# A hybrid decoder layer in which the scheduler orders every engine by its other machine model

## The chip, the cores and the metric

The kernel runs on one core of one Trainium2 chip. Its time is the device time of one execution in microseconds. Before the change it is 1043.64 us, the median of 3 runs (1043.46 to 1045.11). The core has five engines that run beside each other, each with a queue of its own that is worked off strictly in order: TensorE (PE, with its weight loads PEld), VectorE (DVE), ScalarE (ACT), GpSimd (POOL) and SyncE (SP, which here only starts DMAs). They wait for one another by semaphores.

## The reference

One layer over 272 tokens (16 meta tokens and 256 of the sequence), width 2048, in float32:

```
p = h @ W_in -> [q heads | latent kv | indexer q, key, weights | pool channels]
attn = top-64 sparse attention over the latent, T5 bias     (8 heads)
pool = trailing means of 2, 4, 8, 16 tokens less the token, a map per group
h = LN(alpha*h + concat(attn, pool) @ W_o)
z = causal depthwise conv, width 3, of (h @ W_up)           (2 x 5632 columns)
f = (gelu(a) * g) @ W_down                                  (a, g: halves of z)
out = LN(alpha*h + f) without the meta tokens
```

## The kernel before, in words

**Precision and the weight stream.** Every matmul operand is split into a high and a low half, and each product of a weight tile with an activation tile takes three matmuls: high x high (L202), high x low (L203), low x high (L204). All weights come as a stream of 128x2048 tiles of 1 MB. `fetch` (L146 to L163) starts the load of a tile into `wraw` on SP's queue (L149), has ACT copy its two halves of 1024 columns to high parts (L162) and DVE subtract for the low parts (L163), both into `whl`. The pool `wp` has three buffers for each. `weights(ahead=2)` asks for a tile two products before it is used. A load can begin only when the split of the tile three before it has freed `wraw`; a split needs a free `whl`, so the matmuls of the tile three before it must be done.

**Stages in time.** First the keys and latents, from tiles that bring x and weights together. Then 24 projection tiles and, between them, the indexer's dots and top-k, and per head `softmax`, `turn` (L492 to L509, transposes on PE and copies) and `values` (L511 to L520). Then 16 output tiles of W_o (`output`). The sums for LN1 are gathered by the way in `about_k` (L625 to L645; sums on POOL, L635 to L637).

**The folded products.** So that PE need not wait for LN1, the first eight products of the FFN, four columns tiles in two halves each (FOLDED = 4), run on the values before LN1, called `fold`, and are corrected afterwards. During the first of them PE also does the token sums (`deviation`, L244), DVE and POOL make 1/deviation and mean from them (L672 to L679), PE spreads these over the partitions (`deviation_rows`, L250), and ACT copies the spread rows to `rs` and `m2`, which the profile calls `of_token` (L685). After that:

```
def unfold(ps):
    nc.vector.tensor_copy(sc, ps[:, NQ:NE])                        # L719
    nc.vector.tensor_tensor(u, ps[:, :NQ], rs, op=ALU.mult)        # L721
    nc.scalar.activation(w, m2, AF.Identity, bias=sc[:, 1:], scale=sc[:, :1])
    nc.gpsimd.tensor_tensor(u, u, w, op=ALU.add)                   # L724
```

`unfold` reads a folded product's PSUM bank; L721 is the last to do so. There are four such banks (`pm`, tag mm), so a product's matmuls can start only when the unfold of the product four before it is through L721. The conv (ACT L711, DVE L712 and L713), the gate (L728, DVE L729) and the halves of the result (L734, L735) follow; `u` has two buffers. Meanwhile `normalise` makes the sixteen tiles of h for the products that come after: POOL L693 (x times rs), DVE L694 (plus m2), ACT, then DVE L698 (low half, tile `hp`). Sixteen 32x32-block transposes of the residual (L861, DVE) belong to the same stretch.

**The FFN** then alternates up tiles (48 matmuls of 258 columns) with down tiles, which follow a seven-product scheme in kinds A, B and C. A B tile is combined first (DVE L157 to L159) and has a split of 1024 and one of 512 columns. At the end of a group the products in PSUM are added on DVE (L791, L798 to L809) and by DMA.

**The end.** The last part's down product (`down`, L886 to L888) takes rows 0 to 127 in four banks, then rows 128 to 255 in five pieces (three of 512 columns, two of 256). DVE adds each piece to the residual (L892), ACT squares it (L895); the mean comes from the first three pieces (L914, L909) and the product with the weight sums; then (x - mean) g (L900) of all five pieces, the variance (L914, L968, L969), its power -1/2 on POOL (L929 for the first half of the rows, L970 for the second), and x rstd + b (L904) with the output DMAs (L905).

**What sets the order.** The kernel is written for a scheduler: the program's lines say what depends on what, in an order; the scheduler of `TileContext` then orders the instructions of every engine, hands out the pool buffers, and sets the semaphores. It does so by a model of the machine. L1034 opens this context.

## Time and profile before

| | |
|---|---|
| median of 3 runs | 1043.64 us |
| the profiled execution, time | 1044.78 us |
| its span in the profile | 1043.0 us |
| mean granted clock of TensorE | 0.996 |
| matmuls that PE ran, with the short ones | 7649 |
| weight splits on DVE, L163 | 492.8 us, 418 of 1214 ns |
| weight copies on ACT, L162 | 404.4 us, 418 of 1014 ns |
| HBM | 225 GB/s over the span |

A row of the timeline has start, length, engine, line, operation, the tile written and the tiles read (without buffer numbers), shapes and a count of equal operations in a row; in brackets the idle time of the engine before it and what ended it. In the windows each engine's busy time is followed by its count; the last three numbers are TensorE's granted clock (1 is full), the DMA engines' busy share and GB/s. Matmul ends are modelled and overlap, so the pace of PE is read from start to start.

### The profile page before, as it was taken

Reading aid. Unit: us, or ns where it says so; the run is one execution under the profiler, and the core shown is the slowest. Engines: PE = TensorE matmul, PEld = TensorE weight load, DVE = VectorE, ACT = ScalarE, POOL = GpSimd, SP = SyncE. Lnnn points to the kernel's source line nnn. Section 1 sums busy time; section 2 is a strip of 40 time slices with the busy share of each in tenths; the row PEclk is TensorE's granted clock in tenths of the full one; section 3 lists DMA queues with packets and bytes.
Section 4 is the critical chain, followed back from the end, with each engine's and each line's share of the span. In section 5 each row is a group of like instructions: output and inputs, shape, how many; then the busy total and the mean of one; then the engine's idle time right before and its main releaser. Section 6 shows DMA issues by size and latency. Waiting matters only on the chain.

```text
span 1043.0 us, 19170 instructions
## 1 busy us (share of the span) xinstructions
PE 1027.7 (99%) x7649; PEld 975.8 (94%) x7649; DVE 889.4 (85%) x1376; ACT 612.5 (59%) x987; POOL 204.1 (20%) x256
## 2 busy tenths in 40 slices
PE   9999999999999999999999999999999999999996
PEld 8998999999999999999999999999999999999885
DVE  6879468858879987898999999899899999899866
ACT  6666345645447765656566665556556665566543
POOL 1100014125445231201112021120111211111010
PEclk9999999999999999999999999999999999999998
DMA  8756542454552577899788787887879879788872
GB/s 320 260 177 232 197 157 94 142 196 163 198 202 82 202 219 213 268 301 296 264 274 298 290 277 268 292 281 277 277 268 301 282 270 296 267 277 285 306 230 82
DMA packets 59466, 249.75 MB, mean 239 GB/s; under 512 B 21702, under 2 KB 22384, under 8 KB 32368
## 3 DMA queue, kind: packets, MB, share of 16 engines
q1 hardware_dynamic: 34448, 230.15, 61.0%
q0 software_dynamic: 7600, 15.62, 7.9%
q10 hardware_dynamic: 17328, 2.75, 1.5%
q8 instruction: 60, 0.98, 0.4%
q14 instruction: 30, 0.25, 0.1%
HBM read 232.50 MB, written 2.11 MB: 225 GB/s over the span
## 4 chain that ended last, share of the span: by engine, by line
PE 78%; DVE 12%; DMA 4%; issue 2%; ACT 2%; POOL 1%; SPq 0%; DVEq 0%; POOLq 0%; ACTq 0%
PE mm L204 19%; PE mm L203 19%; PE mm L202 19%; PE at L784 5%; PE at L785 5%; PE at L783 5%; DVE whl L163 5%; DMA wraw<-in_w_down 1%; DMA wraw<-in_w_up 1%; ACT whl L162 1%; DMA wraw<-in_w_first 1%; DVE hp L698 1%; DVE x L694 1%; DMA wraw<-in_w_proj 0%; DVE za L712 0%
## 5 line engine op out<-in xcount | busy, mean ns | idle before, releaser
L163 DVE TENSOR_TENSOR whl<-wraw,whl 128x1024 fp32r<-128x1024 f32 (+1 forms) x418 | 492.8, 1214 | 53.6 <-ACT whl L162 51.0
L162 ACT ACTIVATE whl<-wraw 128x1024 fp32r<-128x1024 f32 (+1 forms) x418 | 404.4, 1014 | 142.1 <-DVE wraw L158 41.3
L204 PE MATMUL mm<-hp,whl 128*128 128x258 f32 x1280 | 361.6, 282 | 0.8 <-DVE whl L163 0.8
L203 PE MATMUL mm<-hp,whl 128*128 128x258 f32 x1280 | 360.3, 281 | 0.0
L202 PE MATMUL mm<-hp,whl 128*128 128x258 f32 x1280 | 356.3, 278 | 0.7 <-ACT whl L162 0.7
L202 PEld LDWEIGHTS mm<-hp,whl 128*128 128x128 f32 x1280 | 241.4, 189 | 4.1 <-ACT whl L162 0.9
L203 PEld LDWEIGHTS mm<-hp,whl 128*128 128x128 f32 x1280 | 240.4, 188 | 3.1
L204 PEld LDWEIGHTS mm<-hp,whl 128*128 128x128 f32 x1280 | 241.0, 188 | 1.0 <-DVE whl L163 1.0
L202 PE MATMUL mm<-xp,whl 128*128 128x256 f32 (+5 forms) x384 | 110.4, 287 | 0.0
L204 PE MATMUL mm<-xp,whl 128*128 128x256 f32 (+5 forms) x384 | 108.4, 282 | 0.5 <-DVE whl L163 0.5
L203 PE MATMUL mm<-xp,whl 128*128 128x256 f32 (+5 forms) x384 | 108.2, 282 | 0.0
L783 PE MATMUL at<-whl,gp 128*128 128x512 f32 x212 | 83.5, 394 | 0.5 <-DVE u L808 0.5
L784 PE MATMUL at<-whl,gp 128*128 128x512 f32 x212 | 83.7, 395 | 0.1
L785 PE MATMUL at<-whl,gp 128*128 128x512 f32 x212 | 83.5, 394 | 0.0
L203 PEld LDWEIGHTS mm<-xp,whl 128*128 128x128 f32 x384 | 72.2, 188 | 0.8 <-issue 0.5
L204 PEld LDWEIGHTS mm<-xp,whl 128*128 128x128 f32 x384 | 72.1, 188 | 0.9 <-DVE whl L163 0.9
L202 PEld LDWEIGHTS mm<-xp,whl 128*128 128x128 f32 x384 | 72.2, 188 | 0.6
L711 ACT ACTIVATE z<-mm,cv 128x256 f32<-128x256 f32 x40 | 22.6, 565 | 77.5 <-PE mm L204 77.5
L751 POOL TENSOR_TENSOR forms<-za 128x128 f32<-128x128 f32 x20 | 19.1, 955 | 223.8 <-DVE za L729 216.3
L711 ACT ACTIVATE za<-mm,cv 128x256 f32<-128x256 f32 x40 | 22.5, 562 | 47.4 <-PE mm L204 44.2
L785 PEld LDWEIGHTS at<-whl,gp 128*128 128x128 f32 x212 | 39.8, 188 | 9.2
L783 PEld LDWEIGHTS at<-whl,gp 128*128 128x128 f32 x212 | 39.8, 188 | 8.8 <-DVE u L808 1.0
(307 smaller groups left out, 1850.3 us busy)
## 6 DMA issues: line engine op xcount, KB each, us to landing
wraw<-in_w_up SPq DMA_DIRECT2D x88, 1024.0 KB, 5.1
wraw<-in_w_down SPq DMA_DIRECT2D x80, 1024.0 KB, 6.4
wraw<-in_w_proj SPq DMA_DIRECT2D x24, 1024.0 KB, 4.9
wraw<-in_w_o SPq DMA_DIRECT2D x16, 1024.0 KB, 4.9
y<-v POOLq DMA_DIRECT2D x27, 256.0 KB, 9.2
y<-u POOLq DMA_DIRECT2D x18, 256.0 KB, 4.6
wraw<-in_w_first SPq DMA_DIRECT2D x9, 304.0 KB, 5.3
x<-in_xt SPq DMA_DIRECT2D x1, 2176.0 KB, 8.7
```

The lines of the kernel that those rows point to most:

```text
L162: nc.scalar.activation(hl[:, 0, c], raw[:, c], AF.Copy)
L163: nc.vector.tensor_tensor(hl[:, 1, c], raw[:, c], hl[:, 0, c].bitcast(F32), op=ALU.subtract)
L202: nc.tensor.matmul(ps, wh, ah, start=n == 0, stop=False)
L203: nc.tensor.matmul(ps, wh, al, start=False, stop=False)
L204: nc.tensor.matmul(ps, wl, ah, start=False, stop=n == KT - 1)
L694: nc.vector.tensor_tensor(yd, yd, m2, op=ALU.add)
L698: nc.vector.tensor_tensor(a[:, 1, :NQ], yd, a[:, 0, :NQ].bitcast(F32), op=ALU.subtract)
L711: nc.scalar.activation(z, src[:, 2:NQ], AF.Identity, bias=col(C_B, j), scale=col(C_W, 3 * j + 2))
L751: nc.gpsimd.tensor_tensor(s[:, 3], a11, a21, op=ALU.subtract)
L783: nc.tensor.matmul(ps, a[:, 0, i], hl[:, 0, w], start=fresh, stop=False)
L784: nc.tensor.matmul(ps, a[:, 0, i], hl[:, 1, w], start=False, stop=False)
L785: nc.tensor.matmul(ps, a[:, 1, i], hl[:, 0, w], start=False, stop=last)
```

## The change

One argument is added where the scheduler's context is opened:

```
-    with tile.TileContext(nc) as tc:
+    with tile.TileContext(nc, schedule_with_timeline_sim=True) as tc:
         tile_layer(tc, *args)
```

The scheduler orders all engines' instructions by its other model of the machine, the one that follows queues and transfers in time. No line of the computation changes; every engine has the same operations, in another order, with other buffers of the pools and so other waits. Three places follow as they stand in the two programs (the number behind a name tells buffers apart).

**TensorE, the first folded product.** `st` holds 1/deviation and mean; the two spreads L250 of them are read by ACT as rs and m2. Before, they follow each other:

```order
L203 MATMUL mm<-fold,whl 128x260
L204 MATMUL mm<-fold,whl 128x260
L250 MATMUL at<-ident,st 128x128 x2
L250 MATMUL at<-ident,st 128x2
L250 MATMUL at<-ident,st 128x128 x2
L250 MATMUL at<-ident,st 128x2
L202 MATMUL mm<-fold,whl 128x260
```

Now, at the same step:

```order
L202 MATMUL mm<-fold,whl 128x260
L250 MATMUL at<-ident,st 128x128 x2
L250 MATMUL at<-ident,st 128x2
L203 MATMUL mm<-fold,whl 128x260
L204 MATMUL mm<-fold,whl 128x260
L202 MATMUL mm<-fold,whl 128x260
L203 MATMUL mm<-fold,whl 128x260
L204 MATMUL mm<-fold,whl 128x260
L250 MATMUL at<-ident,st 128x128 x2
L250 MATMUL at<-ident,st 128x2
L202 MATMUL mm<-fold,whl 128x260
```

The spreads are five matmuls apart, and both are later: counted from the first matmul on `fold`, before there are 21 matmuls, the sums L244 (twice three), 21 matmuls, and the spreads; now 36, three L244, 6, three L244, 37, three L250, 5 and three L250.

**VectorE, the unfold of the fourth folded product.** mm_4070 is the bank that the eighth folded product takes next, u_4149 what L721 writes. Before:

```order
L163 TENSOR_TENSOR whl_4064<-wraw_4063,whl_4064 128x1024 x2
L698 TENSOR_TENSOR hp_4122<-x_1154,hp_4122 128x258
L698 TENSOR_TENSOR hp_4128<-x_1154,hp_4128 128x258
L719 COPY sc_4147<-mm_4070 128x2
L721 TENSOR_TENSOR u_4149<-mm_4070,of_token_2766 128x258
L861 STREAM_TRANSPOSE x_1154<-x_1154 128x256
L698 TENSOR_TENSOR hp_4134<-x_1154,hp_4134 128x258
```

Now:

```order
L713 SCALAR_TENSOR_TENSOR z_3983<-u_3978,cv_191,z_3983 128x256
L163 TENSOR_TENSOR whl_4236<-wraw_4235,whl_4236 128x1024
L861 STREAM_TRANSPOSE x_1154<-x_1154 128x256
L698 TENSOR_TENSOR hp_4232<-x_1154,hp_4232 128x258
L861 STREAM_TRANSPOSE x_1154<-x_1154 128x256
L698 TENSOR_TENSOR hp_4294<-x_1154,hp_4294 128x258
L163 TENSOR_TENSOR whl_4321<-wraw_4320,whl_4321 128x1024 x2
L729 TENSOR_TENSOR za_3789<-za_3789,z_3983 128x256
L721 TENSOR_TENSOR u_4149<-mm_4070,of_token_2766 128x258
L712 SCALAR_TENSOR_TENSOR za_3789<-u_4139,cv_191,za_3789 128x256
```

L721 stood behind the splits of whl_4064; now it stands behind those of whl_4162, whl_4236 and whl_4321, three weight tiles further on, and behind fourteen of the transposes L861, of which none was ahead of it before. In the same way u_4139, which empties the third product's bank, stands behind both splits of whl_4162 now, and before behind those of whl_3990.

**VectorE, the end.** y2 is the residual, at_11602, at_11625 and at_11641 are the third, fourth and fifth piece, few holds mean and rstd. Before:

```order
L892 SCALAR_TENSOR_TENSOR y2_3788,row_sums_11478<-y2_3788,at_11602 128x512
L914 TENSOR_REDUCE few_11480<-row_sums_11478 128x1
L892 SCALAR_TENSOR_TENSOR y2_3788,row_sums_11478<-y2_3788,at_11625 128x256
L909 TENSOR_SCALAR few_11480<-few_11480 128x1
L900 SCALAR_TENSOR_TENSOR y2_3788<-y2_3788,few_11480,gb_11443 128x512
L900 SCALAR_TENSOR_TENSOR y2_3788<-y2_3788,few_11480,gb_11445 128x512
L900 SCALAR_TENSOR_TENSOR y2_3788<-y2_3788,few_11480,gb_11447 128x512
L892 SCALAR_TENSOR_TENSOR y2_3788,row_sums_11478<-y2_3788,at_11641 128x256
```

Now:

```order
L892 SCALAR_TENSOR_TENSOR y2_3788,row_sums_11478<-y2_3788,at_11602 128x512
L892 SCALAR_TENSOR_TENSOR y2_3788,row_sums_11478<-y2_3788,at_11625 128x256
L892 SCALAR_TENSOR_TENSOR y2_3788,row_sums_11478<-y2_3788,at_11641 128x256
L914 TENSOR_REDUCE few_11480<-row_sums_11478 128x1
L909 TENSOR_SCALAR few_11480<-few_11480 128x1
L900 SCALAR_TENSOR_TENSOR y2_3788<-y2_3788,few_11480,gb_11443 128x512
L900 SCALAR_TENSOR_TENSOR y2_3788<-y2_3788,few_11480,gb_11445 128x512
L900 SCALAR_TENSOR_TENSOR y2_3788<-y2_3788,few_11480,gb_11447 128x512
```

The add of the last piece stood behind the mean and the three L900; now it stands ahead of them. A little earlier, the L909 that POOL's L929 waits for stood ahead of the add of the second piece, and stands behind it now.

Elsewhere the moves are of one kind each. In the attention, PE does the transposes of a head (L494) and its values (L514) about 45 matmuls of the projection later. In the FFN, of the 36 B tiles 17 have their second split (512 columns) behind both splits of the next up tile and one L157, where at most one split stood between, and PE takes the matmuls with that last part of the tile among those of the next up tile. At the last group but one, L808 and L809 stand ahead of a weight split behind which they stood. SP loads the columns of constants (`cv`) before the last three tiles of the first stage instead of after them.

## The prediction

> **What bounds the kernel now.** The first part of the page gives the busy shares:
>
> ```profile
> span 1043.0 us, 19170 instructions
> PE 1027.7 (99%) x7649; PEld 975.8 (94%) x7649; DVE 889.4 (85%) x1376; ACT 612.5 (59%) x987; POOL 204.1 (20%) x256
> ```
>
> The execution took 1044.78 us, 1.8 us more than its span, and 1.1 us more than the median of the three runs, 1043.64. I add my terms to the profiled execution, 1044.78, and carry the sum over to the median unchanged. TensorE is busy for 99% of the span, so a new order cannot gain much: it can only remove what PE loses, at most the span less 1027.7, which is 15.3 us, and some 10 us of that is the end, when VectorE finishes the last rows after the last matmul. What an order can do is make PE wait. So I looked for the places where it already waits or nearly does. The table of PE's waits has these two, each once:
>
> ```profile
> PE at L514 <- DVE ptx L508: 0.6, 1, 0.6
> PE at L783 <- DVE u L808: 0.5, 1, 0.5
> ```
>
> Next, the windows: busy time of PE, PEld, DVE, ACT and POOL, then PE's granted clock, in a stretch in which PE works on the eight folded products, and in the FFN:
>
> ```profile
> 320.00:370.00 50.00, 49.71 (x413) 49.28 (x412) 48.19 (x94) 35.14 (x61) 19.30 (x19) 1.00 0.48 164
> ...
> 400.00:975.00 575.00, 575.00 (x4166) 542.77 (x4165) 527.00 (x721) 345.44 (x478) 94.55 (x112) 1.00 0.83 280
> ```
>
> In both, DVE runs close to full too (48.19 of 50, 527 of 575). There it has nothing to spare, and what it does first decides. The timeline shows what follows when it is late, right behind the first stretch. These are PE's rows (start, length, in brackets the wait), and then windows of 2 us of PE alone, with the clock as the third number:
>
> ```profile
> 372.29 0.40 PE L202 MATMUL mm<-hp,whl 128*128 128x258 f32 x1 [0.67 <-ACT whl L162]
> ...
> 373.61 0.39 PE L204 MATMUL mm<-hp,whl 128*128 128x258 f32 x1 [0.81 <-DVE whl L163]
> ```
>
> ```profile
> 374.00:376.00 2.00, 2.00 (x15) 0.72 1.05 149
> 376.00:378.00 2.00, 2.00 (x11) 0.50 0.69 274
> 378.00:380.00 2.00, 2.00 (x18) 0.93 0.72 238
> ```
>
> The two waits are 1.5 us together (1.8 from start to start of the matmuls), and right after them the clock is below 1 for 6 us. That costs 2 x (0.28 + 0.50 + 0.07) = 1.7 us more. So a late weight split costs 3.5 us here: the folded products are the place to watch.
>
> **The change: the folded products.** Work is the same, order is not. I number the folded products p0 to p7; the first normal product is p8. They share four PSUM banks, so p6 (mm_4327) needs the bank that the unfold L721 of p2 (u_4139) reads, p7 (mm_4383) that of p3 (u_4149). First the start, rs and m2 (of_token), on which every unfold and every L694 waits:
>
> ```profile
> 303.63 0.28 PE L202 MATMUL mm<-fold,whl 128*128 128x260 f32 x1
> ...
> 307.13 0.86 PE L244 MATMUL at<-ones,sums 128*128 128x64 f32 x6 [0.23 <-POOL sums L637]
> 310.55 1.86 PE L250 MATMUL at<-ident,st 128*128 128x128 f32 x12
> ...
> 353.76 0.28 PE L202 MATMUL mm<-fold,whl 128*128 128x260 f32 x1
> ...
> 354.48 0.28 PE L202 MATMUL mm<-hp,whl 128*128 128x258 f32 x1
> ```
>
> The last two rows are six matmuls apart, so one takes 0.12 us and a product of 48 takes 5.76. Before, p8 starts at 354.48, so p7 at 348.72 and p6 at 342.96. After, 36 matmuls come before the first sums: 303.63 + 36 x 0.12 = 307.95; the first sums (0.86 as the second), six matmuls (0.7) and the second sums end at 310.4, against 307.99 before. Then 37 matmuls (4.4) before the first spread, where before it took 2.56 from 307.99 to 310.55, so the figures st are ready in time. The first spread (half of 1.86), five matmuls and the second end at 317.3, against 312.41: m2 is 4.9 us later. DVE can't begin L694 before that.
>
> Now DVE's rows of before, from its first L694. I price an operation from its start to the next row's start:
>
> ```profile
> 312.93 3.71 DVE L694 TENSOR_TENSOR x<-x,of_token 128x258 f32<-128x258 f32 x5 [2.49 <-ACT of_token L685]
> ...
> 330.67 0.47 DVE L712 SCALAR_TENSOR_TENSOR z<-u,cv,z 128x256 f32<-128x256 f32 x1
> 331.06 1.22 DVE L163 TENSOR_TENSOR whl<-wraw,whl 128x1024 fp32r<-128x1024 f32 x1
> 332.20 0.47 DVE L713 SCALAR_TENSOR_TENSOR z<-u,cv,z 128x256 f32<-128x256 f32 x1
> ...
> 332.67 0.41 DVE L721 TENSOR_TENSOR u<-mm,of_token 128x258 f32<-128x258 f32 x1
> 333.00 0.41 DVE L729 TENSOR_TENSOR za<-za,z 128x256 f32<-128x256 f32 x1
> 333.33 0.42 DVE L698 TENSOR_TENSOR hp<-x,hp 128x258 fp32r<-128x258 f32 x1
> 333.67 0.75 DVE L694 TENSOR_TENSOR x<-x,of_token 128x258 f32<-128x258 f32 x2
> 334.35 0.75 DVE L698 TENSOR_TENSOR hp<-x,hp 128x258 fp32r<-128x258 f32 x2
> ...
> 339.04 0.43 DVE L861 STREAM_TRANSPOSE x<-x 128x256 f32<-128x256 f32 x1
> 339.40 0.78 DVE L698 TENSOR_TENSOR hp<-x,hp 128x258 fp32r<-128x258 f32 x1
> ```
>
> Conv steps (L712, L713) cost 0.39, a split (L163) 1.14, L721 and L729 0.33, L698 and L694 0.34, L861 0.36. L721 of u_4139 is done at 333.00, 20.07 after the first L694, with 12 L694, 6 L698, 4 L163 and 4 conv steps ahead of it. After, the order puts 16, 11, 6 and 2 ahead of it, and 10 L861 that were behind it: 4 x 0.34 + 5 x 0.34 + 2 x 1.14 - 2 x 0.39 + 10 x 0.36 = +8.1. (The two splits of whl_3893 are moved into the idle time ahead of L694 and are not counted; the first L721 too, -0.4.) So it ends at 333.00 + 4.9 + 8.1 - 0.4 = 345.6, while PE comes to p6 at 342.96: a wait of **2.6 us**. From there to u_4149, which has both splits of whl_4236 and of whl_4321 ahead of it: 4 L163, 5 L698, 4 L861, 2 conv steps, L729, L719 (under 0.1) and itself, 4.6 + 1.7 + 1.4 + 0.8 + 0.4 + 0.3 = 9.2, so 354.8. PE, through with p6 at 345.6 + 5.76 = 351.4, waits **3.4 us**, and p8 starts at 360.6 instead of 354.48: +6.1. The next one, u_4299, has two splits and some 2.4 us ahead of it: 359.5, in time.
>
> What is given back: by then DVE has done the transposes and splits that crowd 355 to 372 before, and both splits of whl_4533, the late ones above, stand ahead of the forms' L735. So the two waits at 372 go, 1.8 us, and the lower clock behind them, 1.7. What comes new is a lower clock behind the new waits: none, once or twice 1.7; by the rows above, 1.8 us of waiting was enough for one, so I take one. Folded products: 6.1 - 1.8 - 1.7 + 1.7 = **+4.3**, from +2.6 without a drop to +6.0 with two; my row-by-row sum for DVE may be 2 us off either way. [...]
>
> **The end.** DVE's rows behind the second piece's matmuls, and PE's last one:
>
> ```profile
> 1027.29 0.69 DVE L892 SCALAR_TENSOR_TENSOR y<-y,at 128x512 f32<-128x512 f32 x1 [0.84 <-PE at L888]
> ...
> 1027.90 2.74 DVE L904 SCALAR_TENSOR_TENSOR y<-y,few,gb 128x512 f32<-128x512 f32 x4
> 1030.56 0.68 DVE L892 SCALAR_TENSOR_TENSOR y<-y,at 128x512 f32<-128x512 f32 x1
> ...
> 1031.48 0.42 DVE L892 SCALAR_TENSOR_TENSOR y<-y,at 128x256 f32<-128x256 f32 x1
> ...
> 1031.83 0.21 DVE L909 TENSOR_SCALAR few<-few 128x1 f32<-128x1 f32 x1
> 1032.15 2.08 DVE L900 SCALAR_TENSOR_TENSOR y<-y,few,gb 128x512 f32<-128x512 f32 x3
> 1034.15 0.41 DVE L892 SCALAR_TENSOR_TENSOR y<-y,at 128x256 f32<-128x256 f32 x1
> ...
> 1034.48 0.48 DVE L900 SCALAR_TENSOR_TENSOR y<-y,few,gb 128x256 f32<-128x256 f32 x1
> ...
> 1035.64 0.15 DVE L969 SCALAR_TENSOR_TENSOR few<-squares,few 128x1 f32<-128x1 f32 x1
> 1036.47 2.87 DVE L904 SCALAR_TENSOR_TENSOR y<-y,few,gb 128x512 f32<-128x512 f32 x5 [0.67 <-POOL few L970]
> ```
>
> ```profile
> 1032.58 0.28 PE L888 MATMUL at<-whl,gp 128*128 128x256 f32 x1
> ```
>
> After, the L909 that POOL's power waits for stands behind the L892 of 1027.29, so L904 x4 starts 0.83 (L969 to L904, the same step) behind 1027.90, at 1028.7, and ends at 1031.4; two L892 (0.7 and 0.35) to 1032.4; the last L892, now next, waits for the last matmul, some 0.4 behind 1032.58, and ends at 1033.3. Only then come the mean and L900 x3: 0.5 for mean and L909, 2.0 for the three to 1035.8, and what took 1.16 from 1034.48 to L969: 1037.0 instead of 1035.64, **+1.4**. Before, the three L900 ran while PE did the last piece; after, they lie behind it. Bounds: 0.8, the pow's delay alone, and 2.0, the three L900.
>
> **The rest.** L808 and L809 stand ahead of a split where L783 waits (-0.5), and PE does the turns and values of a head some 45 matmuls later than before, which covers the wait at L514 (-0.6); each may also give nothing. In the FFN, 17 of 36 weight tiles of kind B get their last split two L163 and one L157 later, some 2.4 + 0.7 = 3 us, which holds their raw buffer that much longer; the tile three on comes that much later. For one of them, at 650 us:
>
> ```profile
> 649.99 2.36 DVE L163 TENSOR_TENSOR whl<-wraw,whl 128x1024 fp32r<-128x1024 f32 x2 [0.31 <-ACT whl L162]
> ...
> 654.77 0.28 PE L204 MATMUL mm<-hp,whl 128*128 128x258 f32 x1
> ```
>
> Its first half is split by 651.2 and used at 654.77: 3.6 us of slack against 3. I take 0, with 0 to +8 (17 times 0.5) as the bound. Sum: 4.3 + 1.4 - 0.5 - 0.6 = +4.6, so 1049.4 for an execution like the profiled one and **1048.2 us** for the median.
>
> **The rivals.** (a) *Faster*: the order is made by a model that follows time, and if DVE reaches u_4139 before 342.96 and u_4149 before 348.72, PE never waits there and only the gains are left: -1.8 - 1.7 - 0.5 - 0.6 + 1.4 = -3.2, 1040.4 us. It is decided by 6 us of DVE work; for it speaks that rs is copied before m2, and that ACT and POOL may set some of before's 20.07 us; against it, DVE was busy throughout. Chance 0.15. (b) *No change*: DVE is 2 us earlier than I sum, and neither wait lowers the clock: 4.1 - 3.5 = +0.6 there, 1044 us with the rest. Chance 0.22. (c) *The FFN's ring*: the slack of 3.6 is the typical one, others have less, and every late B tile stalls PE by half a microsecond: +8, 1056 us. Chance 0.08. That the order doesn't change at all is out: the changed kernel's rows differ. The forecast itself, 1045.7 to 1053, has 0.55.
>
> **How the numbers follow.** 0.2%, about what a measurement of this kernel can tell from no change, is 2.1 us. Slower is the forecast and (c), 0.63; same is (b), 0.22; faster is (a), 0.15. The range leaves out the lower half of (a) and most of (c): its lower end 1041.5, its upper end 1043.64 + 6.0 + 2 + 1.4 = 1053.
>
> **What would show it.** Right: L250 ends near 317; PE's first matmuls of the seventh and eighth folded product have waits of 2 to 4 us on DVE (u or L163) near 343 and 351, with a granted clock under 1 behind at least one; no wait at L202/L204 behind p8; L969 some 1.4 us later against the last matmul. Wrong: no PE wait over 1 us between 340 and 360; or PE waits in the FFN, L204 on L163, again and again.

## The result and the profile after

The changed kernel takes **1054.86 us** (median of 4 runs, 1052.84 to 1055.7) against 1043.55 for the kernel before on the same chip (4 runs, 1042.81 to 1045.11): a ratio of 1.0099 with a 95% interval of 1.0080 to 1.0119, so 11.3 us slower. The forecast was 1048.2, with 1041.5 to 1053 as its range. The direction was right, and the size was less than half of what came. The profiled execution of the changed kernel is the fastest of its four, 1052.84 us with a span of 1051.1, 8.1 more than the span before. The page's first part, after:

```profile
span 1051.1 us, 19160 instructions
PE 1028.1 (98%) x7649; PEld 976.2 (93%) x7649; DVE 885.8 (84%) x1376; ACT 612.5 (58%) x987; POOL 212.2 (20%) x256
```

TensorE does the same 1028 us of work, so all 8 us are time in which it stands or runs at a lower clock (mean granted clock 0.992, before 0.996). The table of PE's waits (us in total, times, longest), where before there was 0.6 at L514 and 0.5 at L783 among the long ones:

```profile
PE mm L202 <- DVE u L721: 6.3, 2, 3.6
...
PE at L784 <- DVE whl L163: 1.2, 3, 0.8
...
PE at L783 <- ACT whl L162: 0.3, 1, 0.3
```

**The folded products.** PE's timeline, after: the sums and the spreads of the figures, the starts of p6 (343.78) and p7 (353.34), with the last matmul ahead of the second wait between them, and p8 (361.81):

```profile
307.00 0.76 PE L244 MATMUL at<-ones,sums 128*128 128x64 f32 x6
...
308.50 0.76 PE L244 MATMUL at<-ones,sums 128*128 128x64 f32 x6
...
315.30 0.92 PE L250 MATMUL at<-ident,st 128*128 128x128 f32 x6
...
343.78 0.36 PE L202 MATMUL mm<-fold,whl 128*128 128x260 f32 x1 [2.78 <-DVE u L721]
...
349.50 0.28 PE L204 MATMUL mm<-fold,whl 128*128 128x260 f32 x1
353.34 0.56 PE L202 MATMUL mm<-fold,whl 128*128 128x260 f32 x1 [3.55 <-DVE u L721]
...
361.81 0.28 PE L202 MATMUL mm<-hp,whl 128*128 128x258 f32 x1
```

The spreads end at 316.2 (forecast 317.3), and p6 and p7 each wait for an unfold: from start to start, less the 0.12 that a matmul takes, 2.95 and 3.7 us (forecast 2.6 and 3.4). p7 takes 8.5 us up to p8 instead of 5.76. The windows of PE say why (busy time and count, granted clock, DMA share, GB/s):

```profile
344.00:346.00 2.00, 2.00 (x18) 1.00 0.86 283
...
352.00:354.00 2.00, 0.66 (x3) 0.59 0.87 258
354.00:356.00 2.00, 2.00 (x11) 0.50 0.85 340
356.00:358.00 2.00, 2.00 (x11) 0.50 1.33 270
358.00:360.00 2.00, 2.00 (x15) 0.70 0.76 260
```

Behind the first wait the clock stays 1.00; behind the second it is 0.50, and p7 loses 8.5 - 5.8 = 2.7 us by it. That is the course of this one execution. In after_again, the same program once more (see the experiments), the wait of p6 is as long and the clock falls behind it already:

```profile
343.84 0.56 PE L202 MATMUL mm<-fold,whl 128*128 128x260 f32 x1 [2.79 <-DVE u L721]
```

```profile
344.00:346.00 2.00, 2.00 (x10) 0.50 1.04 295
```

There p6 runs slower, PE comes later to p7 and waits only 2.04 us, and p8 comes 7.2 us later than before, counted from the first folded matmul, instead of 8.3.

**The FFN.** One place in it, after: DVE's rows from the first split of a B tile (645.82) to its last (650.62), and SP's loads there:

```profile
645.82 1.22 DVE L163 TENSOR_TENSOR whl<-wraw,whl 128x1024 fp32r<-128x1024 f32 x1
...
647.35 2.35 DVE L163 TENSOR_TENSOR whl<-wraw,whl 128x1024 fp32r<-128x1024 f32 x2
650.01 0.69 DVE L157 TENSOR_TENSOR wraw<-wraw 128x512 f32<-128x512 f32 x1 [0.30 <-DMA wraw<-in_w_down]
650.62 0.68 DVE L163 TENSOR_TENSOR whl<-wraw,whl 128x512 fp32r<-128x512 f32 x1
```

```profile
643.12 0.33 SPq L149 DMA_DIRECT2D wraw<-in_w_down  x1
...
651.33 0.33 SPq L149 DMA_DIRECT2D wraw<-in_w_down  x1
```

Between the two halves of the tile stand the next tile's two splits and the L157 of the tile two on, and that L157 waits until its own load, issued at 643.12, has landed; the wait is 0.30 us here. Only when the last split has read the raw buffer, at 651.3, does SP issue the next load of a down tile, 0.03 us later. Before, the same tile's two splits and the next tile's two run as one row of four, with the L157 behind them all:

```profile
640.79 4.10 DVE L163 TENSOR_TENSOR whl<-wraw,whl 128x1024 fp32r<-128x1024 f32 x4 [0.18 <-ACT whl L162]
644.81 0.68 DVE L157 TENSOR_TENSOR wraw<-wraw 128x512 f32<-128x512 f32 x1
```

I call hold the time from the end of a B tile's first split to the end of its last, after which the raw buffer is free. From the timelines its mean is 1.0 us over the 36 B tiles before, and 4.1 us over the late ones after (18, of which 17 have an L157 ahead of the last split): 3 us more. These 17 combinations waited 3.1 us in all for their loads in this execution and 0.2 us in after_again, so most of the hold is work.

The waits of DVE and ACT for the loads have grown over the whole run; the first block is from before, the second from after:

```profile
DVE wraw L157 <- DMA wraw<-in_w_down: 3.9, 3, 2.8
...
ACT whl L162 <- DMA wraw<-in_w_up: 16.9, 19, 2.8
```

```profile
DVE wraw L157 <- DMA wraw<-in_w_down: 13.4, 15, 1.9
...
ACT whl L162 <- DMA wraw<-in_w_up: 63.6, 42, 3.5
```

**The end.** DVE's rows behind the last matmul, which PE starts at 1039.46:

```profile
1039.78 0.42 DVE L892 SCALAR_TENSOR_TENSOR y<-y,at 128x256 f32<-128x256 f32 x1 [0.23 <-PE at L888]
...
1040.38 0.21 DVE L909 TENSOR_SCALAR few<-few 128x1 f32<-128x1 f32 x1
1040.71 2.47 DVE L900 SCALAR_TENSOR_TENSOR y<-y,few,gb 128x512 f32<-128x512 f32 x4
...
1043.75 0.16 DVE L969 SCALAR_TENSOR_TENSOR few<-squares,few 128x1 f32<-128x1 f32 x1
```

```profile
1039.46 0.28 PE L888 MATMUL at<-whl,gp 128*128 128x256 f32 x1
```

The three L900 of 512 columns lie behind the last matmul now, and L969 comes 4.29 us behind it instead of 3.06.

The table puts this by stage, for all kernels traced. Each number is how much later than in the profiled execution of before (in us) a point comes: the first folded matmul (303.63 there), p8 (354.48), the 17th normal product (468.05), the last matmul (1032.58) and the end of the span. "Fold" is from the first column to the third, "FFN" from the third to the fourth. The medians are those of the timed runs; the traced execution is one of them, and not always near the median.

| kernel | median, us | ratio, 95% interval | first fold | p8 | 17th | last matmul | span | fold | FFN |
|---|---|---|---|---|---|---|---|---|---|
| after | 1054.86 | 1.0080 to 1.0119 | -0.96 | +7.32 | +3.27 | +6.88 | +8.09 | +4.23 | +3.61 |
| after_again | 1057.34 | 1.0109 to 1.0136 | -0.91 | +6.26 | +2.21 | +11.22 | +12.45 | +3.12 | +9.01 |
| transposes_last | 1060.32 | 1.0117 to 1.0159 | -1.38 | -2.50 | +2.99 | +16.37 | +17.63 | +4.37 | +13.38 |
| b_split_first | 1048.30 | 1.0029 to 1.0053 | -1.30 | +5.87 | +2.27 | +2.94 | +3.22 | +3.57 | +0.67 |
| tail_as_before | 1052.73 | 1.0062 to 1.0095 | -1.03 | +4.64 | +0.58 | +4.58 | +5.13 | +1.61 | +4.00 |
| all_three | 1048.30 | 1.0017 to 1.0056 | -1.73 | -2.84 | +1.94 | +1.98 | +2.27 | +3.67 | +0.04 |
| late_b_split | 1050.37 | 1.0027 to 1.0075 | -0.16 | -0.18 | -1.71 | +2.11 | +2.05 | -1.55 | +3.82 |
| late_b_split_all | 1064.12 | 1.0145 to 1.0231 | -0.06 | -0.08 | -0.89 | +18.57 | +18.63 | -0.83 | +19.46 |
| forms_later | 1043.24 | 0.9970 to 1.0010 | +0.38 | +0.36 | -0.81 | -0.68 | -0.70 | -1.19 | +0.13 |
| rows_early | 1056.68 | 1.0095 to 1.0151 | -0.94 | +4.27 | +0.21 | +6.58 | +7.80 | +1.15 | +6.37 |
| rows_and_splits | 1047.99 | 1.0024 to 1.0057 | -1.36 | +5.38 | +1.78 | +7.54 | +7.85 | +3.14 | +5.76 |
| combine_behind | 1047.63 | 1.0025 to 1.0056 | -1.53 | +6.69 | +2.63 | +4.77 | +5.76 | +4.16 | +2.14 |
| late_b_combine | 1053.70 | 1.0082 to 1.0111 | +0.88 | +0.86 | +2.26 | +10.49 | +10.52 | +1.38 | +8.23 |
| all_four | 1046.67 | 1.0008 to 1.0036 | -1.56 | -2.37 | -0.26 | +2.10 | +2.35 | +1.30 | +2.36 |
| all_three_again | 1048.39 | 1.0024 to 1.0069 | -1.49 | -2.60 | +1.82 | +1.01 | +1.26 | +3.31 | -0.81 |

For the profiled execution of after this reads: -0.96 by what lies ahead, the attention above all, +4.23 in the folded products and what follows them (forecast +4.3), +3.61 in the FFN (forecast 0), +1.21 at the end (forecast +1.4). The median lies 11.3 above before, 3.2 more than this execution's span; in after_again, whose profile lies at its median, the same parts are -0.91, +3.12, +9.01 and +1.23. So the term that failed is the FFN's, and it varies from run to run by several microseconds; the others are nearer the forecast's. One thing lies in the baseline: the traced execution of before has the drop of the clock at 376 (1.7 us). late_b_split and late_b_split_all have the same order there and the same two waits, and the clock stayed at 1.00 (mean over the span 0.997 in both, 0.996 in before). Against such an execution every fold column would read some 1.6 us more.

### The profile page after: what moved, and what is told of

It reads as the page before. It is cut to its first block, busy times and chain, and to the rows that moved or that the text cites. A ratio compares the mean times of both kernels' runs of the same rounds, so it can differ in the third digit from the quotient of the medians.

```text
span 1051.1 us, 19160 instructions
## 1 busy us (share of the span) xinstructions
PE 1028.1 (98%) x7649; PEld 976.2 (93%) x7649; DVE 885.8 (84%) x1376; ACT 612.5 (58%) x987; POOL 212.2 (20%) x256
## 3 DMA queue, kind: packets, MB, share of 16 engines
HBM read 232.50 MB, written 2.11 MB: 223 GB/s over the span
## 4 chain that ended last, share of the span: by engine, by line
PE 58%; DVE 21%; DMA 15%; issue 3%; ACT 2%; POOL 1%; SPq 0%; DVEq 0%; POOLq 0%; ACTq 0%
PE mm L204 15%; PE mm L203 14%; PE mm L202 14%; DVE whl L163 12%; DMA wraw<-in_w_down 10%; DMA wraw<-in_w_up 3%; PE at L784 3%; PE at L785 3%; PE at L783 3%; DVE y L791 1%; DMA wraw<-in_w_first 1%; ACT whl L162 1%; POOL forms L748 1%; DVE x L694 1%; DVE z L712 1%
## 5 line engine op out<-in xcount | busy, mean ns | idle before, releaser
L163 DVE TENSOR_TENSOR whl<-wraw,whl 128x1024 fp32r<-128x1024 f32 (+1 forms) x418 | 498.2, 1219 | 54.5 <-ACT whl L162 53.1
L162 ACT ACTIVATE whl<-wraw 128x1024 fp32r<-128x1024 f32 (+1 forms) x418 | 404.7, 1015 | 215.3 <-DMA wraw<-in_w_up 63.6
L202 PE MATMUL mm<-hp,whl 128*128 128x258 f32 x1280 | 355.6, 278 | 0.0
L202 PEld LDWEIGHTS mm<-hp,whl 128*128 128x128 f32 x1280 | 240.6, 188 | 3.6
L202 PE MATMUL mm<-xp,whl 128*128 128x256 f32 (+5 forms) x384 | 109.7, 286 | 0.0
L784 PE MATMUL at<-whl,gp 128*128 128x512 f32 x212 | 84.3, 398 | 1.0 <-DVE whl L163 0.9
L785 PE MATMUL at<-whl,gp 128*128 128x512 f32 x212 | 83.4, 393 | 0.0
L783 PE MATMUL at<-whl,gp 128*128 128x512 f32 x212 | 80.3, 395 | 0.3 <-ACT whl L162 0.3
L202 PEld LDWEIGHTS mm<-xp,whl 128*128 128x128 f32 x384 | 72.1, 188 | 0.6
L784 PEld LDWEIGHTS at<-whl,gp 128*128 128x128 f32 x212 | 39.9, 188 | 8.8 <-DVE whl L163 1.6
L785 PEld LDWEIGHTS at<-whl,gp 128*128 128x128 f32 x212 | 39.8, 188 | 8.5
L783 PEld LDWEIGHTS at<-whl,gp 128*128 128x128 f32 x212 | 39.4, 188 | 8.8 <-ACT whl L162 1.2
```

The source lines that it names most:

```text
L162: nc.scalar.activation(hl[:, 0, c], raw[:, c], AF.Copy)
L163: nc.vector.tensor_tensor(hl[:, 1, c], raw[:, c], hl[:, 0, c].bitcast(F32), op=ALU.subtract)
L202: nc.tensor.matmul(ps, wh, ah, start=n == 0, stop=False)
L783: nc.tensor.matmul(ps, a[:, 0, i], hl[:, 0, w], start=fresh, stop=False)
L784: nc.tensor.matmul(ps, a[:, 0, i], hl[:, 1, w], start=False, stop=False)
L785: nc.tensor.matmul(ps, a[:, 1, i], hl[:, 0, w], start=False, stop=last)
```

## The experiments

Theory: three rules of the new order cost the time, each by itself. Transposes L861 ahead of the unfolds L721 make p6 and p7 wait; the late last split of B tiles holds raw buffers, so that loads come late and PE stalls in the FFN; the adds ahead of L900 lengthen the end. Rivals: the figures (m2) that come later, not the transposes, cost the folded products; in the FFN it is PE that comes to the held half of the tile itself, and the ring of loads is innocent. All experiments pin the order of single instructions on one engine by this helper, which adds no wait, and the scheduler orders the rest around it; so line numbers are 5 or more higher there (L202 is L207, L784 is L789 or L793):

```
+    def behind(later, first):
+        tc.add_manual_dep(later.ins, first.ins.name,
+                          mybir.DependencyInfo(mybir.DependencyClass.NoSync, mybir.DependencyReason.DATA),
+                          reason="order")
```

### The changed kernel again, and three rules undone one by one

**after_again** is the changed kernel without an edit, on the chip of the next three.

> The changed kernel once more, for the spread of its runs (1052.8 to 1055.7 so far) and a second trace. Theory: the spread is that of the FFN, where the lead of the splits is too short for a slow load: the stalls there fall at other tiles, 3 to 6 us in all, and the rest of the execution repeats the first trace within 0.3 us. Rival: the spread is the granted clock or the start; then the FFN repeats the first trace, tile by tile.

It gave 1057.34 us (1055.45 to 1058.06), 12.6 above before there. The FFN lost 9.0 us in the trace, more than the 3 to 6 expected, and the fold column differs from the first trace by 1.1 us, by the other course of the clock.

**b_split_first** puts the splits of each tile behind the last split of a B tile ahead of it, as before had it:

```
+            for one, last in zip((high, low), state.get("last_of_b", ())):
+                behind(one, last)
+        state["last_of_b"] = (high, low) if kind == "B" else ()
```

> The changed kernel, but in fetch the copies and splits of the tile behind a B tile stand behind the B tile's last copy and split, as before the change. Theory: the late last split holds the raw buffer some 3 us, the loads run later, the splits lose about 2 us of their lead over TensorE, and TensorE then stalls wherever a load is slow. With it undone the FFN's stalls (3 to 5 us) go: 1049.5 to 1051.5 us, the lead over L204 back to 3 to 7 us. Rival: the FFN's stalls come from something else in the new order (the place of the P4 matmuls on TensorE, or slow loads by chance): 1054 to 1056 us, stalls as before.

1048.30 us (1047.85 to 1049.89): 9.0 of the 12.6 us are gone, 1.2 more than expected, and in the traced execution the FFN loses 0.7 instead of 9.0. The last split of B tiles, and what the scheduler orders along with it, is the largest part of the loss. Along with it PE takes the last matmuls of a B tile together again, and DVE's adds at the end have their old place without an edit there: from the last matmul to the end the trace loses 0.3 us instead of 1.2, so 0.9 of the 9.0 belongs to the end.

**transposes_last** puts the transposes behind the last unfold:

```
-                nc.vector.transpose(y[:, m, NM:], y[:, m, NM:])
+                behind(nc.vector.transpose(y[:, m, NM:], y[:, m, NM:]), state["unfolded"])
```

> The changed kernel, but the sixteen transposes L861 stand behind the L721 of the last folded product. Theory: they are what makes the unfolds late: 10 of them 3.6 us for the third product's, 14 of them 5.0 us for the fourth's. The waits of 2.95 and 3.71 us before the seventh and eighth folded product go, and the lower clock behind them (1.6): 6 to 8 us less, 1047 to 1049 us; the transposes may cost 0 to 2 us behind, ahead of the split of whl_4533. Rival: the unfolds are late because m2 comes 4.9 us later; then the waits shrink by 1 to 3 us at most: 1052 to 1054 us.

1060.32 us (1054.5 to 1062.41; the traced one is the slowest), above the theory's range and the rival's. Both waits for unfolds are gone, and p8 comes 2.5 us earlier than before's: the transposes did cause those waits. But the time didn't fall. PE's timeline and windows of this kernel, some 30 us further on:

```profile
393.42 0.40 PE L207 MATMUL mm<-hp,whl 128*128 128x258 f32 x1 [1.54 <-ACT whl L167]
...
394.68 0.39 PE L209 MATMUL mm<-hp,whl 128*128 128x258 f32 x1 [0.75 <-DVE whl L168]
...
409.00 0.49 PE L788 MATMUL at<-whl,gp 128*128 128x512 f32 x1 [1.05 <-ACT whl L167]
...
410.45 0.50 PE L789 MATMUL at<-whl,gp 128*128 128x512 f32 x1 [0.95 <-DVE whl L168]
```

```profile
394.00:396.00 2.00, 1.32 (x7) 0.74 0.81 87
396.00:398.00 2.00, 2.00 (x11) 0.50 0.86 117
...
408.00:410.00 2.00, 0.49 (x1) 1.00 1.27 192
410.00:412.00 2.00, 1.55 (x7) 1.00 0.48 66
```

The weight splits are late now: by the 17th normal product 5.5 us have been lost again, and the fold column reads +4.37 as in after. And the FFN, where this edit changes nothing in the order, loses 13.4 instead of 9.0; some 1.7 of that, by the price of before's drop, is a drop of the clock at 582.7 (0.99 over 470 to 700 us, in after_again 1.00), behind a wait of 2.27. PE had been standing in the folded products while loads and splits ran on (in after DVE is busy for 19.02 of the 20 us from 340 to 360); without that the FFN begins with less in hand, as the lead below shows (0.9 us from 400 to 465 us, where after has 4.7).

**tail_as_before** gives the end its old order on DVE (the add of the second piece behind L909, that of the fifth behind the third L900):

```
-        add(1, c, a, b, ps[:, :b - a])
+        added = add(1, c, a, b, ps[:, :b - a])
+        if c in (1, 4):
+            behind(added, state["scalar"] if c == 1 else scaled_by_g)
```

> The changed kernel, but on VectorE the add of the second piece stands behind the L909 of the first half's variance, and the add of the last piece behind the three L900 of 512 columns, as before the change. Theory: the time from the last matmul to the end goes back from 11.6 to 10.4 us: 1053.7 us. Rival: the seven matmuls of the first piece that TensorE does ahead of the last banks shift the whole chain; then it stays at 11.6: 1054.9 us.

DVE's rows and PE's last matmul of this kernel:

```profile
1037.26 2.08 DVE L906 SCALAR_TENSOR_TENSOR y<-y,few,gb 128x512 f32<-128x512 f32 x3
1039.25 0.42 DVE L897 SCALAR_TENSOR_TENSOR y<-y,at 128x256 f32<-128x256 f32 x1
...
1040.75 0.15 DVE L977 SCALAR_TENSOR_TENSOR few<-squares,few 128x1 f32<-128x1 f32 x1
```

```profile
1037.16 0.28 PE L893 MATMUL at<-whl,gp 128*128 128x256 f32 x1
```

The mean's last step (L969 of before, here L977) comes 3.59 behind the last matmul instead of 4.29, and from the last matmul to the end of the span it is 10.9 us, against 11.6 in after and 10.4 before. So the order of DVE gives 0.7 of the end's 1.2. The other 0.5 stays open. The median, 1052.73 (1049.91 to 1055.53, but for one execution of 4197 us), lies 4.6 below after_again, though the two programs have the same order everywhere but at the end: the rest is scatter, in these two traces 4.0 against 9.0 in the FFN and 1.6 against 3.1 in the fold column.

**all_three** has the three edits together.

> The changed kernel with all three undone at once: the tile behind a B tile behind its last copy and split, the transposes behind the last folded unfold, the adds of the end as before the change. Theory (three separate terms, and a ring of raw buffers that binds only with the late split): the first normal product starts 2.5 us earlier than before the change, as with the transposes alone, the FFN loses 1 to 3 us against before, the end nothing: 1042 to 1045 us, the same as before or 0.2% less. Rival: without the waits at the folded products the stream has too little lead also with the early split, and TensorE stalls through the FFN: 1048 us and more.

1048.30 us (12 runs, 1046.35 to 1051.35), no better than b_split_first alone, where three separate terms should have given 1042 to 1045. It is the rival's time but not its mechanism: the FFN loses nothing in the trace. What is left is the +3.67 of the fold column, which the transposes don't bring back; up to 1.7 of it is a drop of the clock at 408.8 (0.91 over 400 to 420 us), between two waits for splits (1.89 and 0.95 us).

### The late splits alone, put into the kernel before

**late_b_split** is the kernel before, with the last split of every second B tile behind the next tile's two; **late_b_split_all** does it for all B tiles. PE keeps the order of before (in the second nearly).

```
+        for last, one in zip(state.get("last_of_b", ()), (high, low)):
+            behind(last, one)
+        state["b"] = state.get("b", 0) + (kind == "B")
+        state["last_of_b"] = (high, low) if kind == "B" and state["b"] % 2 == 0 else ()
```

> The kernel before the change, with one thing of the change: the last copy and split of every second B tile (18 of 36) stand behind both copies and splits of the next tile. Theory (the ring binds): each of them holds its raw buffer 2.5 to 3 us longer, that lengthens one of the three chains load - split - next load, 18 x 2.7 / 3 = 16 us over the FFN, of which the lead of some 4 us and what slack the chains have are taken off: 1050 to 1058 us, with waits for copies and splits of the tiles that follow, more and more towards the end. Rival (TensorE only waits for the late low half itself, where it needs it): at most 18 x 0.3 = 5 us, all at L784: 1044 to 1049 us.

> As the one before, with all 36 B tiles. Theory (the ring binds): the chains are 32 us longer instead of 16; once the slack is used up every further late split counts in full: some 16 us more than with 18 tiles. Rival (own low half): twice the 18 tiles' loss, at most 10 us.

The first gave 1050.37 us (12 runs, 1045.75 to 1054.02; the traced one is among the fastest), 6.3 above before, the second 1064.12 (1061.06 to 1067.21), 13.8 more, near the theory's 16. So the order of splits alone, with PE's order untouched, costs several microseconds. But in the second PE's table of waits has one row that after has only three times:

```profile
PE at L793 <- DVE whl L168: 11.3, 24, 1.0
```

That is the rival's mechanism: PE comes to the held half itself. It decides where PE keeps the old order; in after PE takes that half later, among the matmuls of the next up tile, and there this wait is 1.2 us in all. So the two kernels show that late splits cost time, not by which way in after.

**forms_later** tries a gain on the kernel before: the low halves of the first two forms behind the next tile's split, against the 1.5 us of waits at 372.

```
+        for low_of_form in state.pop("forms", ()):
+            behind(low_of_form, low)
```

> The kernel before the change, with one thing of the change: the low halves of the first two forms (L735) stand behind the splits of the tile fetched next, so that these no longer wait behind them at 368 to 374 us. Theory (the forms' wait for ScalarE and GpSimd made the split of whl_4533 late, 1.8 us of waits and 1.7 us by the lower clock): 3 to 3.5 us less than before the change, 1040.5 us. Rival: the split is late because VectorE is full there; then the wait moves to the next tile, 1043 to 1044 us.

1043.24 us, a ratio of 0.999 (0.997 to 1.001): no gain that is proven. One of the two waits is left (0.76 us at 373.2). PE stays at full clock there (1.00 in each window from 370 to 380 us), and eight products behind p8 it is 2.0 us ahead; but late_b_split, without this edit, keeps the full clock too and is 1.7 ahead. A wait of 0.8 us at L784 behind it takes more than half of the 2.0 back.

### Which part of the late splits, and what the figures cost

**combine_behind** is the changed kernel with only this edit: the first combination of a tile (L154 or L157) behind the last split of the B tile two ahead. The last split of B stays behind the next tile's two splits, so PE's and ACT's part of the rule stays (PE takes such a tile's last two matmuls three matmuls earlier); only the combination, with its wait for a landing, is taken out of the way of the release.

```
+        if kind in ("A", "B") and len(lows) > 2 and lows[-3]:
+            behind(combined, lows[-3])
```

**rows_early** is the changed kernel with the figures' sums and spreads at before's place among PE's folded matmuls; the order of the FFN stays that of after, so it serves as the other's control on the same chip:

```
+            for one in three if state.get("first") else ():
+                behind(one, state["first"])
```

> The changed kernel, but the first combination (L154 or L157) of the tile two behind a B tile stands behind the B tile's last split; the splits of the tile between stay ahead of it. Theory A (the raw buffer's release waits for the landing of the tile two behind it, so that only one load can run): most of the FFN's loss goes, 1048 to 1050 us. Theory B (it is the two splits, 2.4 us, by which the release is late): little goes, 1053 to 1057 us.

> The changed kernel, but TensorE does the sums L244 and the spreads L250 behind 21 and 42 matmuls of the first folded product, as before the change. Theory (the late m2 costs the stretch from the folded products to 468 us some 4 us, because VectorE is idle for it and full afterwards; taking away the waits of the unfolds alone only moved the loss to 391 to 409 us): TensorE reaches 468 us of before at +0.5 to +1.5 instead of +2.2 to +3.3, with waits at the seventh and eighth product of 2 to 4 us in all instead of 5 to 7; the FFN behind stays as after the change, so 1053 to 1055 us in all. Rival (the order of the transposes, not m2, costs it): waits and times as after the change, 1055 to 1057 us.

combine_behind: 1047.63 us (1046.72 to 1051.07); rows_early: 1056.68 (1052.57 to 1062.31, but for one execution of 5772 us, and the traced one is the fastest). 9.0 us lie between them, as much as b_split_first saved, and after_again, at +12.6, lies as high as rows_early. So it is the combination ahead of the release that makes the FFN slow. DVE's rows of the same place, with L157 and L163 as L162 and L168: the last split is the third of three in a row, and the combination follows it.

```profile
649.32 2.95 DVE L168 TENSOR_TENSOR whl<-wraw,whl 128x1024 fp32r<-128x1024 f32 x3
652.19 0.68 DVE L162 TENSOR_TENSOR wraw<-wraw 128x512 f32<-128x512 f32 x1
```

The hold is 3.1 us here instead of 4.1: 0.6 of the difference is the combination's own work, the rest idle time of DVE. The theory spoke of the wait for the landing, and that is not what the traces show: ahead of the late splits it was 3.1 us in all in after, 0.2 in after_again and 0.8 in rows_early, which lost 9.0 and 6.4 in the FFN. What the two kernels differ in is one microsecond of hold at each of 17 tiles. Both engines' waits for loads are hardly lower in combine_behind (ACT 59.1 us for `in_w_up`, DVE 13.3 at the line that is L157), and b_split_first has 13.4 there too, so those rows are not the measure of it. How the microsecond becomes 9 isn't shown; the lead, told next, gives a part.

**late_b_combine** goes the other way: late_b_split, and the last split of those tiles behind the first combination two on as well.

> The kernel before the change with the late last split of every second B tile, now also behind the first combination of the tile two behind it, as after the change. Theory A: clearly worse than without that (1050.4 us): 1054 to 1062 us. Theory B: one operation of 0.7 us more, 1050 to 1053 us.

1053.70 us (1052.99 to 1056.11), 9.7 above before, 3.3 more than late_b_split, with a ratio (1.0082 to 1.0111) whose interval doesn't meet that of late_b_split (1.0027 to 1.0075). It lies between the two theories' ranges. The combination ahead of the release costs time with PE's old order as well; the hold is 4.4 us against 3.3.

From the timelines of DVE and PE I worked out how far ahead the weight stream runs: for every weight tile used between 400 and 980 us the time from the end of its first split to its first matmul, as a mean.

| kernel | hold, us | lead, us | FFN in the trace | median above before there |
|---|---|---|---|---|
| before | 1.0 | 3.78 | 0 | 0 |
| late_b_split | 3.3 | 3.64 | +3.8 | +6.3 |
| late_b_combine | 4.4 | 3.67 | +8.2 | +9.7 |
| late_b_split_all | 4.7 | 2.66 | +19.5 | +20.1 |
| b_split_first | 0.8 | 3.01 | +0.7 | +3.5 |
| rows_and_splits | 0.8 | 2.87 | +5.8 | +4.0 |
| all_three_again | 0.8 | 2.61 | -0.8 | +3.8 |
| all_three | 0.8 | 2.56 | 0.0 | +4.2 |
| all_four | 0.8 | 2.39 | +2.4 | +2.1 |
| combine_behind | 3.1 | 2.09 | +2.1 | +3.6 |
| after | 4.1 | 2.21 | +3.6 | +11.3 |
| tail_as_before | 4.1 | 1.98 | +4.0 | +8.0 |
| after_again | 4.1 | 1.60 | +9.0 | +12.6 |
| rows_early | 4.1 | 1.43 | +6.4 | +12.7 |
| transposes_last | 4.2 | 1.22 | +13.4 | +15.5 |

The hold is the mean of the late B tiles, or of all where none is late. The first four kernels have PE's old order; there each step of the hold costs time, and the lead says little, since PE itself waits for the held half. Among the others the medians fall into two groups, +2 to +4 with a hold of up to 3.1 us and +8 to +16 with 4.1 or more. In the traces the FFN's loss falls by and large as the lead grows; rows_and_splits stands outside, and combine_behind has no longer a lead than after, though its median is 8 to 9 us better (its traced execution, 1050.51, is one of its two slowest). In after the lead shrinks along the way: by stretches of 65 us from 400 us on it is 4.7, 3.6, 3.4, 2.0, 1.5, 1.5, 1.0, 1.0 and 1.2, and the stalls come from about 700 us on. Before it stays between 3.0 and 4.8. transposes_last begins with 0.9 and stalls throughout.

**rows_and_splits** has the early figures, b_split_first and the old end; **all_four** the transposes last as well; **all_three_again** is all_three beside it.

> The same, and also the tile behind a B tile behind its last copy and split, and the adds of the end as before the change. Theory: the three losses are named; what is left is 0.5 to 1.5 us at the folded products, 1 us in the FFN, 0.5 us at the end, and a gain of 1 to 1.7 us in the attention that is in the first of these: 1044 to 1047 us. Rival: the FFN loses for another reason once the lead is short: 1048 us and more.

> The changed kernel with everything undone that has been named: rows of TensorE early, transposes behind the last folded unfold, the tile behind a B tile behind its last split, the adds of the end as before. Theory (the late m2 is what costs the stretch from the first folded matmul to 468 us): that stretch is 0 to 1.5 us longer than before the change, where it was 3.7 us longer with the late rows, and the whole takes 1043 to 1046 us, 2 to 4 us less than with three undone. Rival (the order of VectorE's work in that stretch costs it, whenever it starts): the stretch stays 3 to 4.5 us longer, 1047 to 1050 us.

> The kernel with three undone once more, on the same chip beside the one before, for the comparison: 1046 to 1050 us, the stretch from the first folded matmul to 468 us 3 to 4.5 us longer than before the change. If it is under 2 us here, executions differ there by as much as the rows are thought to cost, and the two can't be told apart by single traces.

rows_and_splits: 1047.99 us (10 runs, 1044.82 to 1052.86; the traced one, 1052.6, has 5.6 us at 662 to 727 that no edit explains). all_four: 1046.67 (12 runs, 1043.55 to 1049.86). all_three_again: 1048.39 (12 runs, 1045.75 to 1057.75). The first is at the rival's lower end, the second just above the theory's range. Between the last two the medians differ by 1.7, with intervals that overlap, and the fold column by 2.0 (+1.30 against +3.31). Up to 1.7 of the 2.0 is one drop of the clock (all_three_again, at 409.0), which all_four doesn't have (mean granted clock 0.995 against 0.997). Early figures alone gave +1.15 in rows_early and +3.14 in rows_and_splits, and there too the traces differ by one drop (0.995 against 0.991, of which one drop, at 718 to 724 us, lies behind that stretch). So what the late figures cost isn't settled. all_four is the best with the new model and still 2.1 us slower than before (1.0008 to 1.0036). No version beat the kernel before.

## Why the prediction was wrong in size

**The folded products, +4.3: right in place and in the cause of the waits; in sum partly by luck.** Both waits came at p6 and p7, and in after on L721, each 0.3 us longer than worked out. transposes_last has neither, so the transposes are a cause. What the late m2 adds isn't shown: counted from the first folded matmul DVE begins L694 4.8 us later, as forecast (4.9), and at its old time in rows_early, but the order behind it changed there too, and the two unfolds end only 0.2 and 0.4 us earlier. "I take one" drop of the clock was right in number in this trace, behind the second wait only; after_again has two. Its price was mis-sized: 2.7 us instead of 1.7. How the drops fall differed between executions, as the last section shows: with the same order of the stretch the column reads +4.23, +3.12 and +1.61 (after, after_again, tail_as_before), and the drop of before at 376 (0.50) that "goes" did not come behind the same waits in late_b_split (1.00). Against it stood small stalls of before that I didn't count and that are gone: 0.23 at the sums, 0.4 at a late split, and 0.3 at 348.8, some 1 us in all. Before:

```profile
336.96 0.39 PE L204 MATMUL mm<-fold,whl 128*128 128x260 f32 x1 [0.26 <-DVE whl L163]
```

So p8 comes 8.3 us later, counted from the first folded matmul: 6.67 of waits, 2.7 of clock, less 1.1. The gain behind it came as well: no wait of PE's is left between 361 and 470 us, and 4.1 us of the 8.3 are back by the 17th normal product (forecast 3.5). The length of a wait alone didn't tell whether the clock falls: by the profile's idle times 2.78 us in after brought no drop and 3.55 one, in after_again waits of 2.79 and 2.04 each brought one, and behind before's two pieces of 1.5 together the clock fell to 0.50.

What I had not seen there is that the waits are also a rest for the weight stream. Where transposes_last takes them away, as much is lost again from 391 us on, at late splits (5.5 us by the 17th normal product). I worked out what is late next for before's waits, not for the new ones.

**The end, +1.4: right**, +1.2 in both traces of the changed kernel. The add that waits for the last matmul and the L900 behind it came as described; undone, they give 0.7.

**The rest, -1.1**: PE's two waits at L514 and L783 are gone from the table of after, and the attention brings -0.96 at the first folded matmul, of which some 0.6 was forecast.

**The FFN, taken as 0: this step failed.** I wrote "some 2.4 + 0.7 = 3 us, which holds their raw buffer that much longer", and set it against "3.6 us of slack" of one tile. The 3 us were right: the mean hold went from 1.0 to 4.1 us. The slack was wrong in two ways. It was read at one tile. Before's own trace has, from the end of the first split to the first matmul of the tile three on from each of the 18 B tiles that became late, between 0.3 and 6.0 us, and under 3.0 at ten of them (3.3 by this measure at the tile I chose). And slack isn't given anew for each tile: the lead shrinks in the course of after from 4.7 us to 1.0, and the stalls begin where it is spent. That the combination ahead of the release, and with it the last microsecond of hold, makes the loss, combine_behind shows (with 3.1 us instead of 4.1 the kernel takes 1047.6 instead of 1056.7), and late_b_combine in the other direction. Of what is lost this way the table of PE's waits names only 1.5 us in after; the rest are gaps too short for it, seen only from start to start, which is why I read the FFN by the stage table.

With about 7 us for this term (the 11.3 of the median, less 4.2 and 1.2, with the attention's gain of 1.0 added) the sum would have been right. Rival (c) named the place, and its +8, 17 times half a microsecond, comes near the size; its mechanism, each late tile stalling PE by itself, is that of late_b_split_all, not that of after, where only a few stalls are at L784. I gave it 0.08, since one slack of 3.6 stood against 3.

**Open**: by what way one microsecond of hold costs 9 us, since waits for loads and lead hardly differ; 1.3 us in the fold stretch of all_four, where transposes, figures and splits are as before (some 3 against an execution of before without the drop); half a microsecond of the end; how much of late_b_split's +6.3 is PE's own wait and how much the ring, since its traced execution lost 1.2 us by about 500 us, then nothing until about 983.

## What to carry to other kernels

When an order moves the last reader of a ring buffer, add up how long the buffer is held now, with each instruction ahead of that reader. Compare it with the slack of every tile that takes such a buffer next, not of one: here the slack went from 0.3 to 6.0 us, and the last microsecond of hold, one instruction in the way, cost most of the loss (9.0 us between rows_early and combine_behind). In a stream that runs for 600 us read the lead along the whole stage. And where a stall is removed ahead of such a stream, look whether it comes back behind, as 5.5 us did in transposes_last.

## What the runs showed of the hardware that was not expected

In these runs the granted clock didn't follow the length of a wait alone: behind nearly the same waits it fell in one execution and not in another. The same two waits at 372 (0.67 to 0.68 and 0.81 to 0.83 us) were followed by 0.50 in before and late_b_combine and left 1.00 in late_b_split and late_b_split_all. For late_b_split:

```profile
373.43 0.39 PE L213 MATMUL mm<-hp,whl 128*128 128x258 f32 x1 [0.83 <-DVE whl L168]
```

```profile
374.00:376.00 2.00, 2.00 (x19) 1.00 0.91 129
```

The wait at p6 was 2.78 us in after and 2.79 in after_again, two executions of one program; from 344 to 346 us the clock was 1.00 in the first and 0.50 in the second. In transposes_last waits of 1.54 and 0.75 us were followed by 0.50 (396 to 398 us), and waits of 1.05 and 0.95 us left 1.00 (408 to 424 us). What decides whether it falls isn't shown.

And the same order of instructions scattered by several microseconds where the weight stream has little lead: after and after_again, the same program, traced at 1052.84 and 1057.2 us, with +3.6 and +9.0 in the FFN.
